# A four-layer encoder on one core: eight pairs of projection groups for six, earlier splits of score banks, and scoring in smaller steps

## The chip, the cores and the metric

The kernel runs on one core of a Trainium2 chip. A core has five engines that work side by side, each with its own instruction stream in a fixed order: TensorE (PE in the profile, with its weight loads shown as PEld), VectorE (DVE), ScalarE (ACT), GpSimd (POOL) and SyncE (SP), whose stream here only issues transfers. Sixteen DMA engines move data between the chip's memory (HBM) and the core's SBUF. The metric is the device time of one execution in microseconds (us); lower is better.

## The reference

Four layers act on a residual stream `x` of 256 tokens by 2048 features, all in float32. Layers 0 and 3 use windowed grouped-query attention, layer 1 a neighbourhood attention on a token grid, layer 2 a differential attention.

```python
for i in range(4):
    h = rmsnorm(x, norm_pre[i])
    proj = h @ w_in[i]             # 2048 x 5120 in layers 0 and 3, 2048 x 8192 in layers 1 and 2
    q, k, v, g = split(proj)
    o = attention_i(q, k, v)       # 16 heads or score maps; one kind of three
    y = (o * silu(g)) @ w_out[i]   # 2048 x 2048
    x = x + rmsnorm(y, norm_post[i])
    x = x + sigmoid(x @ pe_gate[i]) * (p[i] @ pe_proj[i])
```

## The kernel before, in words

**Products in three parts.** Every float32 operand is split into a high part (ACT, a copy into a rounded form) and a low part (DVE, a subtraction): `split`, L108 to L115. `mm3` (L117 to L120) then issues three matmuls: high by high, high by low, low by high. Weights come from HBM in chunks of 128 x 1024 (512 KB), which hold two steps of the contraction for 512 output columns. Tile `wr` holds a raw chunk, `wh` and `wl` its halves.

**Groups and pairs.** A group is 512 output columns: eight chunks, two halves of tokens, so 8 x 2 x 2 x 3 = 96 matmuls of 128 x 512. A group is named by what it yields: `q1` is the second group of queries. Two groups can be joined to a `Pair`, which computes the 2 x 2 block product with seven block products instead of eight: 28 pair chunks of six matmuls. The names are P1 to P7 and E, four chunks each. The weights of P1 and P3 come by a plain transfer into tile `wc`. Those of P5, P7 and P6 are made in place: POOL issues a DMA that adds another block to the tile that has just been split (L228), so P1 is followed by P5, and P3 by P7 and then P6, in the same tile. For E a raw chunk is added by DVE (L221). The order is

```python
PAIR = [("P1", 0), ("P1", 1), ("P1", 2), ("P1", 3), ("P2", 0), ("P5", 0), ("P5", 1), ("P5", 2), ("P5", 3),
        ("P2", 1), ("P2", 2), ("P2", 3)] + [(n, c) for n in ("P3", "P7", "P6", "E") for c in range(4)]
```

**The order of the stream.** `ORDERS` (L42) says for each kind of layer which two groups open it, which pairs follow with which plain groups laid between their chunks, and over how many of those plain chunks the pair is spread (the last number of an entry), and which groups close it. `layer_plan` lays three pair chunks after each eighth plain chunk and spreads the rest evenly over the others. A pair occupies three PSUM banks (`sacc`), plain groups two (`acc`) or two of the three; three more banks (`ps`) serve transposes, scores and values.

**Splits ahead.** The split of a chunk is written four places of the stream ahead of its products (`AHEAD_SPLIT`), in five buffers, so ACT waits until PE has finished the oldest one. There are four buffers each for `wr` and `wc`.

**Steps.** Everything else (attention, transposes, norms) is a queue of short steps. `run_stream` runs one step per plain chunk or per two pair chunks (two when the queue is long). The attention of four heads or maps is started when its q, k and v have arrived: `attend` and `attend_diff`. In them a step `score(p)` makes the scores of two heads or maps, `soft` the exponentials on ACT, `scale` or `blend` the normalisation, `trans` the transposes of the probabilities with their split into `pth` and `ptl`, `value` the product with v. The scheduler of the framework orders each engine's instructions by the place in the program; `tc.high_priority()` lets instructions go ahead of others that are also possible then.

Of the kernel before, what the change touches and what calls it, by code (L numbers as in the profile page):

```python
# [10 lines left out]
F32 = mybir.dt.float32  # L11
# [3 lines left out]
ALU = mybir.AluOpType  # L15
# [24 lines left out]


ORDERS = {  # L42
    0: (["k0", "v0"], [(("q1", "q2"), ["q0", "q3", "g0"], 22)], ["g3", "g1", "g2"]),
    1: (["k0", "q0"], [(("k1", "q1"), ["v0", "v1", "g0"], 22), (("k2", "q2"), ["v2", "g1", "k3"], 20)],
        ["q3", "v3", "g2", "g3"]),
}
ORDERS[2] = ORDERS[1]

# [6 lines left out]
def alibi_slope(h, n):  # L55
    return 2.0 ** (-8.0 * (h + 1) / n)
# [36 lines left out]
def encoder_kernel(ctx: ExitStack, tc: tile.TileContext, t, out):  # L93
# [14 lines left out]
    def split(dst_h, dst_l, src, scale=None):  # L108
        if scale is None:
            A.activation(dst_h, src, AF.Copy)  # L110
            V.tensor_sub(dst_l, src, dst_h.bitcast(F32))  # L111
        else:
            A.activation(dst_h, src, AF.Copy, scale=scale)
            V.scalar_tensor_tensor(dst_l, src, scale, dst_h.bitcast(F32),
                                   op0=ALU.mult, op1=ALU.subtract)  # L115

    def mm3(acc, lh, ll, rh, rl, start, stop, **kw):  # L117
        PE.matmul(acc, lh, rh, start=start, stop=False, **kw)  # L118
# [312 lines left out]
    def acts_of(acts, kt, layer=None, u=None, gain=True):  # L431

        def step():
            if layer is None:
                split(acts.pair(kt, 0), acts.pair(kt, 1), turned(xn[kt // 8], kt % 8 // 2))
                acts.done(kt)
                return
            c = kt % 4
            if not layer:
                for a in range(2):  # L440
                    split(*acts.part(kt + a), u[kt // 4][:, c + a], scale=gpre[:, 0, kt + a:kt + a + 1])
                acts.done(kt)
                return
            ps = turned(xn[kt // 8], kt % 8 // 2)
            if c == 0:
                u.append(work.tile([P, 4, S], F32, name=("s", "snat")[kt // 8]))
            for a in range(2):
                A.activation(u[kt // 4][:, c + a], ps[:, a], AF.Copy, scale=gpre[:, layer, kt + a:kt + a + 1])
            split(acts.pair(kt, 0), acts.pair(kt, 1), u[kt // 4][:, c:c + 2])
            acts.done(kt)  # L450
        return step
# [41 lines left out]
    def turn_heads(dst, i, nat, flag, minus=False):  # L493

        scale = (DH ** -0.5 if i == 1 else 1.0) * (-1 if minus else 1)

        def turn(p):
            def step():
                if not dst:
                    name, bufs = ("kv", 4) if i == 0 else ("q", 2)  # L500
                    for _ in range(2):
                        dst.append(work.tile([P, 4, S], F32R, name=name, bufs=bufs))
                ps = turned(nat, p)
                c = slice(2 * p, 2 * p + 2)
                split(dst[0][:, c], dst[1][:, c], ps, scale=None if scale == 1.0 else scale)
                if p == 1:
                    flags[flag] -= 1
            return step

        flags[flag] = flags.get(flag, 0) + 1  # L510
        steps.extend([idle, turn(0), turn(1)])
# [45 lines left out]
    def turned(nat, p):  # L557

        ps = psp.tile([P, 2, S], F32, name="ps")
        for a in range(2):  # L560
            for m in range(T):
                PE.transpose(ps[:, a, m * P:(m + 1) * P],  # L562
                             nat[:, m, (2 * p + a) * P:(2 * p + a + 1) * P], ident)
        return ps
# [24 lines left out]
    def scores(q, k, qi, ki):  # L589
        ps = psp.tile([P, T, S], F32, name="ps")  # L590
        for m in range(T):
            r = (slice(None), qi, slice(m * P, (m + 1) * P))
            mm3(ps[:, m], q[0][r], q[1][r], k[0][:, ki], k[1][:, ki], True, True)
        return ps

    def probs_T(src_of):

        ps = psp.tile([P, T, S], F32, name="ps")
        for kt in range(T):
            for m in range(T):  # L600
                PE.transpose(ps[:, kt, m * P:(m + 1) * P], src_of(m)[:, kt * P:(kt + 1) * P], ident)  # L601
        h = work.tile([P, T, S], F32R, name="pth")
        l = work.tile([P, T, S], F32R, name="ptl")
        split(h, l, ps)
        return h, l

    def exponentials(s, sink_of=None):
# [17 lines left out]
    def attend(j, q, k, v, k_of, bias_of, sink_of, gs, og_of, after_scores):  # L625

        s = [None, None]
        sums, pt = {}, {}

        def score(p):  # L630
            def step():
                s[p] = work.tile([P, 4, S], F32, name="s")
                for a in range(2):
                    i = 2 * p + a
                    bias_of(s[p][:, a * T:(a + 1) * T], scores(q, k, i, k_of(i)), i)
            return step

        def soft(p):
            def step():
                sums[p] = exponentials(s[p], sink_of(p) if sink_of else None)  # L640
            return step

        def scale(p):
            def step():
                sm, es = sums[p]
                if es is not None:
                    V.tensor_add(sm, sm, es)
                rc = small.tile([P, 4], F32, name="rc")
                V.reciprocal(rc, sm)
                for e in range(4):  # L650
                    A.activation(s[p][:, e], s[p][:, e], AF.Copy, scale=rc[:, e:e + 1])  # L651
            return step

        def trans(i):
            def step():
                pt[i] = probs_T(lambda m: s[i // 2][:, (i % 2) * T + m])
            return step

        def value(i):
            def step():  # L660
                if i % 2 == 0:
                    pt["ps"] = psp.tile([P, 2, S], F32, name="ps")
                ps, (ph, pl) = pt["ps"], pt.pop(i)
                c = slice(k_of(i) * DH, (k_of(i) + 1) * DH)
                for kt in range(T):
                    mm3(ps[:, i % 2], v[0][:, kt, c], v[1][:, kt, c], ph[:, kt], pl[:, kt],
                        kt == 0, kt == T - 1)
                if i % 2 == 1:
                    c = 4 * (j % 2) + i
                    A.activation(og_of(j)[:, c - 1:c + 1], ps, AF.Copy)  # L670
            return step

        def gate(p):
            def step():
                c = 4 * (j % 2) + 2 * p
                og = og_of(j)[:, c:c + 2]
                V.tensor_mul(og, turned(gs[0], p), og)
                if p == 1:
                    flags["gs"] = 0
            return step  # L680

        def both(*fs):
            return lambda: [f() for f in fs]

        return [score(0), both(soft(0), score(1)), both(scale(0), soft(1), after_scores),
                scale(1), trans(0), trans(1), both(value(0), trans(2)),
                both(value(1), trans(3)), value(2), value(3)], [gate(0), gate(1)]

    def attend_diff(j, q, k, v, dist, subln, nlam, lam_init, gs, og_of, after_scores):
# [2 lines left out]
        o = slice(512 * (j % 2), 512 * (j % 2 + 1))  # L692
        ss = small.tile([P, 2, T], F32, name="ss")

        def score(hd):
            def step():
                s[hd] = work.tile([P, 4, S], F32, name="s")
                for a in range(2):
                    ps = scores(q, k, 2 * hd + a, 2 * hd + a)
                    V.scalar_tensor_tensor(s[hd][:, a * T:(a + 1) * T], dist,  # L700
                                           -alibi_slope(2 * j + hd, 8), ps,
                                           op0=ALU.mult, op1=ALU.add)
            return step

        def soft(hd):
            def step():
                sums[hd] = exponentials(s[hd])[0]
            return step
# [16 lines left out]
        def trans(hd):  # L725
            def step():
                pt[hd] = probs_T(lambda m: s[hd][:, m])
            return step
# [35 lines left out]
        def both(*fs):  # L764
            return lambda: [f() for f in fs]

        return [score(0), both(soft(0), score(1)), both(blend(0), soft(1), after_scores),
                blend(1), trans(0), trans(1), value(0), value(1),
                norm], [gate]

    def lambda_of(layer):
# [14 lines left out]
    def layer_plan(layer, hx, sums, xs_last):  # L786
# [69 lines left out]
        def lo_split(j, p):  # L856
            def step():
                kt = 4 * j + 2 * p
                if kind == 2:
                    src = turned(og_of(j), 2 * (j % 2) + p)  # L860
                else:
                    src = og_of(j)[:, kt % 8:kt % 8 + 2]
                split(lo.pair(kt, 0), lo.pair(kt, 1), src)
                lo.done(kt)
            return step

# [291 lines left out]
```

## Time and profile before

| What | Value |
|---|---|
| Median of 3 runs | 2073.7 us (2073.3 to 2075.14) |
| Profiled execution, its own time | 2073.2 us |
| Its span in the profile | 2071.4 us |
| PE busy | 2043.3 us, 99% |
| DVE busy | 1386.4 us, 67% |
| ACT busy | 1226.9 us, 59% |
| Moved by DMA | 428.63 MB, mean 207 GB/s |

The 1.8 us between time and span lie outside the span. A matmul's bar lasts longer than the distance to the next one's start, so the busy time of PE says when it had work in flight, not how much it did; the distance from start to start does. The clock row grants TensorE its higher level (2.4 GHz, shown as 1.00) in every stretch. The input projections are at 5 to 268 us (layer 0), 462 to 848 us (layer 1), 1042 to 1427 us (layer 2) and 1621 to 1876 us (layer 3); output projection and gate lie between them.

### The profile page before, as it was taken

The page shows a single profiled execution, that of the slowest core. Times are in us where ns is not written, and L with a number is a line of the kernel's source. Part 1 is how long each engine was busy: PE and PEld are TensorE (multiplying, and loading weights), DVE is VectorE, ACT ScalarE, POOL GpSimd, SP SyncE. Part 2 cuts the span into 40 slices and gives each one's busy share as a digit, 9 for nine tenths or more (in the row PEclk, how much of TensorE's full clock was granted, in tenths as well). Part 3 has the DMA queues.
Part 4 walks back from the last instruction along what each step waited for, and adds up shares of the span by engine and source line. Part 5 has one row for each costly group of instructions (what it writes and reads, how often), then busy time and mean ns, then how long its engine had stood idle before and what let it go on. Part 6 is the DMA issues. An engine that isn't in the chain of part 4 may idle for free.

```text
span 2071.4 us, 26023 instructions
## 1 busy us (share of the span) xinstructions
PE 2043.3 (99%) x9675; PEld 1690.6 (82%) x9675; DVE 1386.4 (67%) x1603; ACT 1226.9 (59%) x1802; POOL 76.4 (4%) x98
## 2 busy tenths in 40 slices
PE   9999999999999999999999999999999999999999
PEld 6788888888888888888888887888888888888887
DVE  7667755576777776555667787766556767775554
ACT  8567745465657666444656566555545567774543
POOL 0010000000000100000000101000000001000000
PEclk9999999999999999999999999999999999999999
DMA  8875576466788866564667878655656687456744
GB/s 312 261 189 187 174 231 215 154 213 197 224 263 218 237 222 196 194 223 151 208 205 218 247 234 213 226 192 190 217 165 205 209 235 183 153 172 225 223 152 143
DMA packets 125009, 428.63 MB, mean 207 GB/s; under 512 B 13521, under 2 KB 16209, under 8 KB 124881
## 3 DMA queue, kind: packets, MB, share of 16 engines
q1 hardware_dynamic: 114512, 389.21, 56.8%
q0 software_dynamic: 10368, 37.75, 10.4%
q8 instruction: 76, 1.25, 0.2%
q14 instruction: 53, 0.43, 0.1%
HBM read 418.52 MB, written 8.39 MB: 206 GB/s over the span
## 4 chain that ended last, share of the span: by engine, by line
PE 61%; DVE 3%; issue 3%; ACT 2%; DMA 2%; POOL 0%; DVEq 0%; ACTq 0%; POOLq 0%
PE acc L118 10%; PE acc L120 10%; PE acc L119 10%; PE sacc L118 8%; PE sacc L119 8%; PE sacc L120 8%; DMA wr<-in_w_in 2%; PE ps L562 2%; DVE wl L111 1%; ACT wh L110 1%; PE ps L119 1%; PE ps L120 1%; PE ps L118 1%; PE ps L601 1%; ACT s L651 0%
## 5 line engine op out<-in xcount | busy, mean ns | idle before, releaser
L111 DVE TENSOR_TENSOR wl<-wr,wh 128x1024 fp32r<-128x1024 f32 (+1 forms) x605 | 736.7, 1222 | 434.4 <-ACT wh L110 429.7
L110 ACT ACTIVATE wh<-wr 128x1024 fp32r<-128x1024 f32 (+1 forms) x605 | 639.3, 1058 | 584.1 <-PE acc L120 293.0
L118 PE MATMUL acc<-wh,lh 128*128 128x512 f32 x896 | 354.4, 396 | 1.6 <-ACT wh L110 1.3
L119 PE MATMUL acc<-wl,lh 128*128 128x512 f32 x896 | 350.6, 391 | 4.7 <-DVE wl L111 4.7
L120 PE MATMUL acc<-wh,lh 128*128 128x512 f32 x896 | 350.4, 391 | 0.0
L118 PE MATMUL sacc<-wh,ls 128*128 128x512 f32 x664 | 262.2, 395 | 2.7 <-ACT snat L545 2.1
L119 PE MATMUL sacc<-wl,ls 128*128 128x512 f32 x664 | 259.3, 391 | 0.1
L120 PE MATMUL sacc<-wh,ls 128*128 128x512 f32 x664 | 258.9, 390 | 0.0
L110 ACT ACTIVATE wh<-wc 128x1024 fp32r<-128x1024 f32 x144 | 152.4, 1059 | 140.6 <-PE acc L120 103.3
L111 DVE TENSOR_TENSOR wl<-wc,wh 128x1024 fp32r<-128x1024 f32 x144 | 175.8, 1223 | 81.7 <-ACT wh L110 79.6
L118 PE MATMUL sacc<-wh,lh 128*128 128x512 f32 x528 | 210.0, 398 | 2.2 <-ACT wh L110 2.1
L119 PE MATMUL sacc<-wl,lh 128*128 128x512 f32 x528 | 206.7, 391 | 2.5 <-DVE wl L111 2.5
L120 PE MATMUL sacc<-wh,lh 128*128 128x512 f32 x528 | 206.9, 392 | 0.0
L119 PEld LDWEIGHTS acc<-wl,lh 128*128 128x128 f32 x896 | 168.5, 188 | 39.5 <-DVE wl L111 6.8
L118 PE MATMUL acc<-wh,ls 128*128 128x512 f32 x504 | 197.9, 393 | 0.0
L118 PEld LDWEIGHTS acc<-wh,lh 128*128 128x128 f32 x896 | 168.4, 188 | 36.1 <-ACT wh L110 2.0
L120 PEld LDWEIGHTS acc<-wh,lh 128*128 128x128 f32 x896 | 168.3, 188 | 35.1
L119 PE MATMUL acc<-wl,ls 128*128 128x512 f32 x504 | 196.5, 390 | 0.0
L120 PE MATMUL acc<-wh,ls 128*128 128x512 f32 x504 | 196.3, 390 | 0.0
L118 PEld LDWEIGHTS sacc<-wh,ls 128*128 128x128 f32 x664 | 124.8, 188 | 29.1 <-ACT snat L545 3.0
L120 PEld LDWEIGHTS sacc<-wh,ls 128*128 128x128 f32 x664 | 124.7, 188 | 26.2
L119 PEld LDWEIGHTS sacc<-wl,ls 128*128 128x128 f32 x664 | 124.9, 188 | 24.6 <-DVE wl L111 0.5
(227 smaller groups left out, 2501.4 us busy)
## 6 DMA issues: line engine op xcount, KB each, us to landing
wr<-in_w_in SPq DMA_DIRECT2D x367, 512.0 KB, 4.5
wr<-in_w_out SPq DMA_DIRECT2D x128, 512.0 KB, 4.2
wr<-in_pe_gate SPq DMA_DIRECT2D x128, 512.0 KB, 3.9
wc<-in_w_in POOLq DMA_DIRECT2D x72, 512.0 KB, 7.2
wc<-in_w_in SPq DMA_DIRECT2D x48, 512.0 KB, 4.7
wr<-in_pe_proj SPq DMA_DIRECT2D x16, 512.0 KB, 4.7
xs<-lx SPq DMA_DIRECT2D x12, 512.0 KB, 3.8
lx<-xs SPq DMA_DIRECT2D x12, 512.0 KB, 5.3
```

Source lines behind the costliest of these rows:

```text
L110: A.activation(dst_h, src, AF.Copy)
L111: V.tensor_sub(dst_l, src, dst_h.bitcast(F32))
L118: PE.matmul(acc, lh, rh, start=start, stop=False, **kw)
L119: PE.matmul(acc, lh, rl, start=False, stop=False, **kw)
L120: PE.matmul(acc, ll, rh, start=False, stop=stop, **kw)
L562: PE.transpose(ps[:, a, m * P:(m + 1) * P], nat[:, m, (2 * p + a) * P:(2 * p + a + 1) * P], ident)
L601: PE.transpose(ps[:, kt, m * P:(m + 1) * P], src_of(m)[:, kt * P:(kt + 1) * P], ident)
```

## The change

Three things change. In layers 1 and 2 `ORDERS` now has three pairs (k1 with q1, k2 with q2, k3 with q3) for two, each spread over 15 of the 16 plain chunks beside it; in layers 0 and 3 the one pair is spread over 21 plain chunks instead of 22. Splits whose source is a `ps` bank (and one DVE product from such a bank) are issued with high priority. A scoring step makes one head or map instead of two; the scaling or blending of the second half and the first transposes become one step. From L112 on, lines of the changed kernel have numbers that are 4 to 6 higher.

```diff
 ORDERS = {
-    0: (["k0", "v0"], [(("q1", "q2"), ["q0", "q3", "g0"], 22)], ["g3", "g1", "g2"]),
-    1: (["k0", "q0"], [(("k1", "q1"), ["v0", "v1", "g0"], 22), (("k2", "q2"), ["v2", "g1", "k3"], 20)],
-        ["q3", "v3", "g2", "g3"]),
+    0: (["k0", "v0"], [(("q1", "q2"), ["q0", "q3", "g0"], 21)], ["g3", "g1", "g2"]),
+    1: (["k0", "q0"], [(("k1", "q1"), ["v0", "v1"], 15), (("k2", "q2"), ["g0", "v2"], 15),
+                      (("k3", "q3"), ["g1", "v3"], 15)], ["g2", "g3"]),
 }
...
+    def split_now(*args, **kw):
+        with tc.high_priority():
+            split(*args, **kw)
...
-                split(dst[0][:, c], dst[1][:, c], ps, scale=None if scale == 1.0 else scale)
+                split_now(dst[0][:, c], dst[1][:, c], ps, scale=None if scale == 1.0 else scale)
...
-        split(h, l, ps)
+        split_now(h, l, ps)
...
-        def score(p):
-            def step():
-                s[p] = work.tile([P, 4, S], F32, name="s")
-                for a in range(2):
-                    i = 2 * p + a
-                    bias_of(s[p][:, a * T:(a + 1) * T], scores(q, k, i, k_of(i)), i)
+        def score(p, a):
+            def step():
+                if a == 0:
+                    s[p] = work.tile([P, 4, S], F32, name="s")
+                i = 2 * p + a
+                bias_of(s[p][:, a * T:(a + 1) * T], scores(q, k, i, k_of(i)), i)
...
-        return [score(0), both(soft(0), score(1)), both(scale(0), soft(1), after_scores),
-                scale(1), trans(0), trans(1), both(value(0), trans(2)),
+        return [score(0, 0), score(0, 1), both(soft(0), score(1, 0)), score(1, 1), both(scale(0), soft(1), after_scores),
+                both(scale(1), trans(0)), trans(1), both(value(0), trans(2)),
                 both(value(1), trans(3)), value(2), value(3)], [gate(0), gate(1)]
```

The same is done in `attend_diff`, and the other three uses of `split` on a `ps` bank are replaced too.

Three places show how instructions move. The first is ACT in layer 0, the second attention: `wh` are weight splits, `s` the scores, `pth` the high part of transposed probabilities. Before:

```order
113 L617 ACTIVATE s,sm<-s,ng 128x256 x4
114 L622 ACTIVATE es<-es 128x4
115 L110 ACTIVATE wh<-wr 128x1024
116 L110 ACTIVATE wh<-wc 128x1024
117 L651 ACTIVATE s<-s,rc 128x256 x4
118 L617 ACTIVATE s,sm<-s,ng 128x256 x4
119 L622 ACTIVATE es<-es 128x4
120 L110 ACTIVATE wh<-wc 128x1024
121 L651 ACTIVATE s<-s,rc 128x256 x4
122 L110 ACTIVATE pth<-ps 128x512
123 L110 ACTIVATE wh<-wr 128x1024
124 L110 ACTIVATE pth<-ps 128x512
```

The same place of the changed kernel:

```order
113 L621 ACTIVATE s,sm<-s,ng 128x256 x4
114 L626 ACTIVATE es<-es 128x4
115 L110 ACTIVATE wh<-wr 128x1024
116 L655 ACTIVATE s<-s,rc 128x256 x4
117 L110 ACTIVATE wh<-wr 128x1024
118 L621 ACTIVATE s,sm<-s,ng 128x256 x3
119 L110 ACTIVATE pth<-ps 128x512
120 L621 ACTIVATE s,sm<-s,ng 128x256
121 L626 ACTIVATE es<-es 128x4
122 L110 ACTIVATE wh<-wr 128x1024
123 L655 ACTIVATE s<-s,rc 128x256 x3
124 L110 ACTIVATE pth<-ps 128x512
```

The first `pth` has moved ahead of the last exponential and of the second scaling, which stood before it.

The second is DVE in layer 1 where the first pair ends: `wl<-wr` are splits of plain chunks, `wl<-wc` those of pair chunks, `wc<-wc,wr` the additions for E, `ptl` the low parts of transposed probabilities. Before:

```order
376 L111 TENSOR_TENSOR wl<-wr,wh 128x1024
377 L221 TENSOR_TENSOR wc<-wc,wr 128x1024
378 L111 TENSOR_TENSOR wl<-wc,wh 128x1024
379 L111 TENSOR_TENSOR wl<-wr,wh 128x1024
380 L221 TENSOR_TENSOR wc<-wc,wr 128x1024
381 L111 TENSOR_TENSOR wl<-wc,wh 128x1024
382 L111 TENSOR_TENSOR wl<-wr,wh 128x1024
383 L221 TENSOR_TENSOR wc<-wc,wr 128x1024
384 L111 TENSOR_TENSOR wl<-wc,wh 128x1024
385 L221 TENSOR_TENSOR wc<-wc,wr 128x1024
386 L111 TENSOR_TENSOR wl<-wr,wh 128x1024
387 L111 TENSOR_TENSOR wl<-wc,wh 128x1024 x2
```

The same pair's end in the changed kernel:

```order
358 L225 TENSOR_TENSOR wc<-wc,wr 128x1024
359 L111 TENSOR_TENSOR ptl<-ps,pth 128x512
360 L653 RECIPROCAL rc<-sm 128x4
361 L111 TENSOR_TENSOR wl<-wc,wh 128x1024
362 L111 TENSOR_TENSOR ptl<-ps,pth 128x512
363 L225 TENSOR_TENSOR wc<-wc,wr 128x1024
364 L111 TENSOR_TENSOR wl<-wr,wh 128x1024
365 L111 TENSOR_TENSOR wl<-wc,wh 128x1024
366 L111 TENSOR_TENSOR ptl<-ps,pth 128x512 x2
367 L111 TENSOR_TENSOR wl<-wc,wh 128x1024
368 L225 TENSOR_TENSOR wc<-wc,wr 128x1024
369 L111 TENSOR_TENSOR wl<-wr,wh 128x1024
```

Fewer plain splits stand between the additions, and the four `ptl` of the first attention have come in among them.

The third is POOL in layer 2, which issues the adding DMAs (`wc<-in_w_in2` by its place) and computes a power for the attention's norm (`ro`), in one queue. Before:

```order
22 L420 TENSOR_TENSOR rstd<-v,mhalf 128x2
23 L228 DMA wc<-in_w_in 128x1024 x9
24 L750 TENSOR_TENSOR ro<-ss,mhalf 128x4
25 L228 DMA wc<-in_w_in 128x1024 x7
26 L750 TENSOR_TENSOR ro<-ss,mhalf 128x4
27 L228 DMA wc<-in_w_in 128x1024 x8
28 L750 TENSOR_TENSOR ro<-ss,mhalf 128x4 x2
```

The same stretch of the changed kernel:

```order
22 L424 TENSOR_TENSOR rstd<-v,mhalf 128x2
23 L232 DMA wc<-in_w_in 128x1024 x12
24 L756 TENSOR_TENSOR ro<-ss,mhalf 128x4
25 L232 DMA wc<-in_w_in 128x1024 x9
26 L756 TENSOR_TENSOR ro<-ss,mhalf 128x4
27 L232 DMA wc<-in_w_in 128x1024 x12
28 L756 TENSOR_TENSOR ro<-ss,mhalf 128x4
29 L232 DMA wc<-in_w_in 128x1024 x3
30 L756 TENSOR_TENSOR ro<-ss,mhalf 128x4
```

There are 36 adding DMAs for 24; two of the powers, for one, now stand behind the ninth DMA of a pair with three more of that pair behind them.

## Rows read from the trace of the kernel before

**Rows 1.** The page, part 1: busy time, share of the span, instructions.

```profile
span 2071.4 us, 26023 instructions
PE 2043.3 (99%) x9675; PEld 1690.6 (82%) x9675; DVE 1386.4 (67%) x1603; ACT 1226.9 (59%) x1802; POOL 76.4 (4%) x98
```

**Rows 2.** Windows by stage: length, busy time (instructions) of engines, clock, DMA.

```profile
5.00:268.00 263.00, 254.46 (x1256) 209.94 (x1255) 192.90 (x260) 184.76 (x319) 12.72 (x14) 1.00 0.74 229
268.00:462.00 194.00, 193.69 (x884) 159.59 (x883) 117.02 (x120) 102.08 (x136) 0.72 (x1) 1.00 0.63 200
462.00:848.00 386.00, 381.76 (x1840) 317.92 (x1840) 275.52 (x306) 243.88 (x347) 21.83 (x26) 1.00 0.74 218
...
1042.00:1427.00 385.00, 378.65 (x1807) 313.96 (x1806) 278.62 (x339) 235.40 (x348) 26.26 (x30) 1.00 0.72 216
...
1621.00:1876.00 255.00, 253.47 (x1266) 212.03 (x1265) 181.49 (x231) 168.49 (x275) 11.81 (x14) 1.00 0.66 193
```

**Rows 3.** Timeline of PE from 880 us: start, length, instruction.

```profile
880.02 0.39 PE L118 MATMUL acc<-wh,ls 128*128 128x512 f32 x1
...
892.26 0.39 PE L118 MATMUL acc<-wh,ls 128*128 128x512 f32 x1
```

**Rows 4.** Waits of PE in the whole span: total us, times, longest us.

```profile
PE acc L119 <- DVE wl L111: 4.7, 5, 2.9
PE sacc L119 <- DVE wl L111: 2.5, 3, 1.0
PE sacc L118 <- ACT snat L545: 2.1, 3, 0.7
...
PE ps L118 <- ACT pth L110: 1.5, 2, 0.8
```

**Rows 5.** Groups by form: count | busy us, mean ns | idle before, releasers.

```profile
L111 DVE TENSOR_TENSOR wl<-wr,wh 128x1024 fp32r<-128x1024 f32 x603 | 735.3, 1224 | 433.7 <-ACT wh L110 429.1
L110 ACT ACTIVATE wh<-wr 128x1024 fp32r<-128x1024 f32 x603 | 638.1, 1060 | 583.8 <-PE acc L120 293.0 <-PE sacc L120 230.3 <-issue 40.9
...
L221 DVE TENSOR_TENSOR wc<-wc,wr 128x1024 f32<-128x1024 f32 x24 | 29.2, 1223 | 13.9 <-DMA wr<-in_w_in 13.5
...
L538 DVE SCALAR_TENSOR_TENSOR snat<-sacc,rstd,snat 128x512 f32<-128x512 f32 x24 | 17.4, 745 | 0.0
...
L551 DVE TENSOR_TENSOR snat<-snat 128x512 f32<-128x512 f32 x6 | 4.1, 684 | 0.0
```

**Rows 6.** The adding DMAs (L228): POOL's ns min/median/max, then transfer to landing.

```profile
L228 POOL DMA_DIRECT2D wc<-in_w_in x72: 862/862/1047, 53.1 to 1738.4; - x72
...
DMA to landing us min/median/max: 5.2/7.2/11.3
```

**Rows 7.** Windows inside the pairs' stretches of layers 1 and 2.

```profile
660.00:710.00 50.00, 49.90 (x236) 41.47 (x235) 37.47 (x37) 32.78 (x38) 6.93 (x8) 1.00 0.93 249
...
1190.00:1240.00 50.00, 48.76 (x235) 40.15 (x234) 41.49 (x54) 32.38 (x48) 3.45 (x4) 1.00 0.78 228
1240.00:1290.00 50.00, 48.32 (x220) 38.88 (x218) 34.44 (x37) 32.88 (x44) 7.99 (x9) 1.00 0.83 224
1290.00:1340.00 50.00, 48.12 (x232) 40.02 (x232) 39.94 (x51) 28.99 (x44) 0.00 (x0) 1.00 0.64 221
```

**Rows 8.** Timeline of PE in layer 0, the second attention, with idle time before.

```profile
170.55 0.38 PE L118 MATMUL ps<-pth,kv 128*128 128x256 f32 x1 [0.78 <-ACT pth L110]
171.28 0.38 PE L119 MATMUL ps<-ptl,kv 128*128 128x256 f32 x1 [0.34 <-DVE ptl L111]
```

**Rows 9.** DMA issues: instruction, count, size, median us to landing.

```profile
wc<-in_w_in POOLq DMA_DIRECT2D x72, 512.0 KB, 7.2
```

More of the change, by code (lines that the diff above doesn't have):

```diff
@@ L434, in step @@
             if layer is None:
-                split(acts.pair(kt, 0), acts.pair(kt, 1), turned(xn[kt // 8], kt % 8 // 2))
+                split_now(acts.pair(kt, 0), acts.pair(kt, 1), turned(xn[kt // 8], kt % 8 // 2))
                 acts.done(kt)
@@ L676, in step @@
                 og = og_of(j)[:, c:c + 2]
-                V.tensor_mul(og, turned(gs[0], p), og)
+                ps = turned(gs[0], p)
+                with tc.high_priority():
+                    V.tensor_mul(og, ps, og)
                 if p == 1:
@@ L693, in attend_diff, with score @@
         ss = small.tile([P, 2, T], F32, name="ss")
-        def score(hd):
+        def score(hd, a):
             def step():
[L697 to L702, printed above, removed]
+                if a == 0:
+                    s[hd] = work.tile([P, 4, S], F32, name="s")
+                ps = scores(q, k, 2 * hd + a, 2 * hd + a)
+                V.scalar_tensor_tensor(s[hd][:, a * T:(a + 1) * T], dist,
+                                       -alibi_slope(2 * j + hd, 8), ps,
+                                       op0=ALU.mult, op1=ALU.add)
             return step
@@ L765, in both @@
             return lambda: [f() for f in fs]
-        return [score(0), both(soft(0), score(1)), both(blend(0), soft(1), after_scores),
-                blend(1), trans(0), trans(1), value(0), value(1),
+        return [score(0, 0), score(0, 1), both(soft(0), score(1, 0)), score(1, 1), both(blend(0), soft(1), after_scores),
+                both(blend(1), trans(0)), trans(1), value(0), value(1),
                 norm], [gate]
@@ L862, in step @@
                     src = og_of(j)[:, kt % 8:kt % 8 + 2]
-                split(lo.pair(kt, 0), lo.pair(kt, 1), src)
+                split_now(lo.pair(kt, 0), lo.pair(kt, 1), src)
                 lo.done(kt)
```

## The prediction

> **What bounds the kernel now.** I read the page's first part, then windows by stage, then PE's own waits, then the pairs' stretches. The first part shows PE with work in flight for 2043.3 of 2071.4 us, DVE for 67% and ACT for 59% of the span [rows 1]. PE idles 28.1 us in all. The windows say where [rows 2]: 263.00 - 254.46 = 8.5 us in the input projection of layer 0, 4.2 in that of layer 1, 6.4 in layer 2, 1.5 in layer 3; between layers 0 and 1 only 0.3 in 194 us. So the idle time sits where pairs and attention are mixed, and the rest of the program is a row of matmuls without holes.
>
> What a matmul is worth is not its bar of 0.39 us. From the L118 row at 880.02 to the one at 892.26 there are 54 starts in 12.24 us [rows 3]: 0.2267 us each. A plain chunk (12 matmuls) holds PE for 2.72 us and a pair chunk (6) for 1.36.
>
> **The change part by part.**
>
> *Two more pairs.* Two groups as plain ones are 2 x 96 = 192 matmuls, as a pair 28 x 6 = 168. Two more pairs, one each in layers 1 and 2, take away 48 matmuls of 128 x 512. PE is the engine that everything waits for here, so they count in full: 48 x 0.2267 = 10.9 us. The transposes that turn the results move from `nat` to `snat` with the same count.
>
> The Trainium skill (TensorE: Matmul & The Clock Gate, Back-to-back issue gap) gives about 131 ns for each 512-column matmul in a sustained stream of weight loads and matmuls; the gain would be 48 x 0.131 = 6.3 us by that estimate. The trace does not agree: 226.7 ns in a stretch without a hole [rows 3], and the measurement decides.
>
> *What the pairs add.* Each pair has 28 splits for 16, so 12 more on ACT (1.06 us) and DVE (1.22 us), 4 additions for E (1.22 us) and a longer drain of its banks (4 of 0.745 us and one of 0.684) [rows 5]. DVE gets 12 x 1.224 + 4 x 1.223 + 3.7 = 23.3 us more per layer, ACT 12 x 1.06 = 12.7. DVE in layer 1 then works 275.5 + 23.3 = 298.8 us of about 381 (386 less half of 10.9): 78% after 71% [rows 2]. That lies beside PE's work as long as the splits stay ahead. POOL issues 24 more adding DMAs of 512 KB [rows 9]; plain transfers keep their number, so 12.6 MB more are moved, 3% of 428.6.
>
> *The denser stretch.* Before, 22 pair chunks were spread over 20 or 18 plain chunks; now 25 over 14, 1.79 to one. Four pair chunks and what lies between them last 4 x 1.36 + 2.24 x 2.72 = 11.5 us on PE, where they lasted 14.3 (18 plain) to 15.3 us (20). Three things must fit into these 11.5 us. (a) DVE while E runs: 4 x (1.224 + 1.223) + 2.24 x 1.224 = 12.5 us, so it falls 1.0 us behind; before it needed 13.8 of 14.3. The reserve is the four chunks split ahead, 4 x 11.5/6.24 = 7.4 us of PE's time. (b) One round of the adding chain (split, add, next split of the same tile): 1.06 + 1.22 + 7.2 us to landing at the median [rows 5, 6] = 9.5. It fits by 2 us; with the longest landing, 11.3, it is 13.6 and late by 2.1. (c) DMA: the share was 0.93 at 249 GB/s in the densest 50 us, with PE idle for only 0.1 us of them [rows 7]; the mean over a whole mix changes little, since a third of its plain chunks left with the time.
>
> The price of extra waiting, from both sides. At best none: the densest window of DMA cost PE nothing. From the nearest count: layers 1 and 2 wait 4.2 + 6.4 = 10.6 us with four pairs, 2.65 a pair, so two more cost 5.3. At worst the chain of (b) is late in each round (below). I take 3 us, nearer to the row per pair, because some of today's waits there belong to attention, which gets better.
>
> *Score banks first, one head to a step.* No instruction is added but the steps: one more per attention. PE waits for `pth` and `ptl` at 170.55 and 171.28 us for 0.78 and 0.34 us [rows 8]; the transposed bank stood behind exponentials and scalings on ACT. With the first `pth` moved ahead of them, and the scores of two heads no longer in one burst on DVE, such waits shrink. Their kind totals 1.5 us over the whole span in the row of `pth` [rows 4], and some of the 7.2 us that PE waits for `wl` there stems from the same bursts of scoring. Bounds: a loss of the 1.22 us of a weight split that is now behind, once per attention at worst and only where the reserve of 7.4 us is gone; a gain of at most the 10.0 us of layers 0 and 3, of which the chip's start is a part that stays. I take -2 us. Spreading over 21 instead of 22 plain chunks in layers 0 and 3 leaves PE's work as it is; I cost it at nothing, covered by the same reserve.
>
> *The tail.* With two closing groups for four, less plain work follows the last scores in layers 1 and 2: 16 plain chunks are 43.5 us after the pair's end. The last attention needs about 18 steps (turns, 11 of attention), one or two to a chunk, and its result is first wanted six chunks into the output projection. It fits; no price.
>
> *Sum.* -10.9 + 3 - 2 = -9.9 us on the profiled 2073.2: 2063.3. The median of the runs is 0.5 above the profiled one, so 2063.8, rounded to 2064.
>
> **The rivals.**
>
> *A, the adding chain becomes the bound (slower).* In P7 and P6 a tile's next split needs the landing of a DMA issued one round earlier. If landings go to the 11.3 us of the longest row, each of the two rounds in each of the six pairs of layers 1 and 2 is 2.1 us late; where bursts on DVE have used the reserve, that is 12 x 2.1 = 25 us on PE: 2073.7 - 10.9 + 25.2 = 2088. It turns into a loss from 10.9/12 = 0.9 us late, that is from a mean landing of 11.5 + 0.9 - 2.3 = 10.1 us with the reserve spent. For it: windows near full DMA share exist already [rows 7], POOL's queue holds a norm ahead of three adding DMAs twice in layer 2, and 24 more are issued. Against it: the median is 7.2 and the reserve is 7.4.
>
> The Trainium skill (SBUF — State Buffer, Who interferes with whom) adds that a DVE instruction with two SBUF inputs blocks a GpSimd one that reads SBUF for its whole length, which would speak against more adding DMAs beside more splits; 24 x 1.22 us would be put into the chain by such a block. This trace shows no sign of it: POOL's issue took 862 ns at the least and at the median, 1047 at most [rows 6].
>
> *B, DVE's load eats the gain (about the same).* In 50 us windows with DVE at 80 to 83% PE idled 1.2 to 1.9 us, 2.5 to 3.8% [rows 7]. The three mixes of a layer last about 3 x (16 x 2.72 + 28 x 1.36) = 245 us of dense work and some 27 of attention; both layers 544 us. At 3.8% that is 20.7 us where there are 10.6: +10.1, and 2073.7 - 10.9 + 10.1 = 2072.9. For it: E now asks more of DVE than the time holds, and the first attention falls into it. Against it: the two windows' waits are partly for a bank's drain, not for DVE.
>
> *C, the waits mostly vanish (faster still).* If scoring in small steps takes away half the 20.6 us of idle time in the four projections beside keeping the pairs free, at most some -8 beyond the matmuls: 2073.7 - 10.9 - 8 = 2054.8. Against it: most waits there are single ones under 1 us with a different cause each [rows 4].
>
> *That the pairs don't take the matmuls away* can be left out: the counts above are those of the program.
>
> **How the numbers follow.** The forecast (2064, from 2058 to 2069) 0.64; A 0.09; B, with a half gain, 0.18; C 0.09. Runs of this kernel differ by up to 0.1%, so 0.2% (4.1 us) is about what can be told from no change: faster below 2069.6, slower above 2077.8. Faster is the forecast, C and a third of B: 0.79; same is most of B and the small losses of A: 0.13; slower is the rest of A and of B: 0.08. The range leaves out most of A and the far end of C: 2056 to 2074.
>
> **What would show it.** PE should have 48 fewer matmuls and the same 0.2267 us between starts in a full stretch; DVE about 45 us and ACT about 25 us more busy time; idle time of PE in layers 1 and 2 between 8 and 18 us in sum, in layers 0 and 3 below 9. The waits for `pth` and `ptl` should shrink. A is right if ACT's `wh` waits for the landing of `wc` by tens of us in sum and landings of L232 have a median over 9; B if PE waits for `wl` far longer than 7.2 us while DVE is above 90% in the E stretches. The forecast is wrong if idle time in layers 1 and 2 grows by more than 7 us, or if it falls by more than 6.

## The result and the profile after

The changed kernel takes 2093.62 us (median of 4 runs, 2091.59 to 2095.51; the profiled one took 2095.51) where the kernel before took 2074.42 beside it: 1.0093 times as long, with a 95% interval of [1.0081, 1.0105]. The forecast was 2064 us, in a range of 2056 to 2074. It had the sign wrong.

In rows of the changed kernel the lines from L117 of the kernel before on have numbers that are 4 to 6 higher; L110 to L114 are the same in both. First part of the page of the changed kernel, and its row of the adding DMAs (count, size, median us to landing):

```profile
span 2093.7 us, 26098 instructions
PE 2052.1 (98%) x9627; PEld 1693.1 (81%) x9627; DVE 1433.0 (68%) x1645; ACT 1251.8 (60%) x1826; POOL 98.7 (5%) x122
...
wc<-in_w_in POOLq DMA_DIRECT2D x96, 512.0 KB, 8.0
```

The counts are those forecast: PE has 48 matmuls fewer than in [rows 1], DVE works 46.6 us longer, ACT 24.9, and 24 adding DMAs more are issued. So the work is as expected, and the time was lost beside it. The windows by stage of the changed kernel show where (length; busy us and instructions of PE, PEld, DVE, ACT, POOL; granted clock; DMA share; GB/s):

```profile
5.00:268.00 263.00, 256.71 (x1257) 211.53 (x1256) 195.52 (x260) 184.89 (x319) 12.71 (x14) 0.99 0.74 229
...
462.00:861.00 399.00, 384.96 (x1809) 317.85 (x1808) 295.72 (x323) 254.15 (x356) 32.25 (x38) 0.98 0.80 228
1055.00:1450.00 395.00, 381.18 (x1780) 314.59 (x1779) 296.88 (x353) 245.12 (x347) 37.12 (x41) 0.98 0.80 227
1644.00:1898.00 254.00, 253.89 (x1266) 211.68 (x1265) 184.34 (x232) 168.45 (x275) 11.79 (x14) 1.00 0.65 193
```

Against [rows 2]: layer 0 has the same length, layer 3 is 1 us shorter, layers 1 and 2 are 13 and 10 us longer, although each lost 24 matmuls (5.4 us). Read to a hundredth from the timeline, from their first matmul to the first of the output projection, they are 12.5 and 9.0 longer; the loss to explain is 12.5 + 9.0 + 10.9 = 32.4 us. PE's idle time there is 14.0 + 13.8 = 27.9 us, after 4.2 + 6.4 = 10.6. That is 17.3 of the 32.4. The clock column says where to look for more: 0.98 where it was 1.00.

PE's waits in the changed kernel over the whole span (total us, times, longest us):

```profile
PE ps L566 <- DVE snat L542: 11.0, 8, 3.1
PE acc L123 <- DVE wl L111: 6.7, 6, 2.8
PE sacc L122 <- DVE snat L542: 4.7, 4, 1.3
PE ps L566 <- DVE snat L555: 3.7, 6, 1.5
PE sacc L123 <- DVE wl L111: 2.1, 3, 1.0
```

Three of the five rows have to do with `snat`, the buffer into which a pair's three banks (`sacc`) are drained: 11.0 + 4.7 + 3.7 = 19.4 us. In the kernel before, the same waits (its L562 and L118 behind L538) are 2.0 and 0.6:

```profile
PE ps L562 <- DVE snat L538: 2.0, 3, 1.5
...
PE sacc L118 <- DVE snat L538: 0.6, 2, 0.3
```

The waits for `wl`, at which rival B pointed, grew only from 7.2 to 8.8.

**One pair's end, before and after.** PE's timeline of the kernel before at the first pair's end of layer 1 (start, length, instruction):

```profile
617.74 0.39 PE L120 MATMUL sacc<-wh,lh 128*128 128x512 f32 x1
617.97 0.39 PE L118 MATMUL acc<-wh,lh 128*128 128x512 f32 x1
...
623.41 0.38 PE L562 MATMUL ps<-ident,snat 128*128 128x128 f32 x2
```

E's last matmul into `sacc` starts at 617.74. Two plain chunks into `acc` follow, 24 matmuls, and at 623.41 the first transposes that turn `snat` find their data (a later one waits 0.25 us). PE worked for 5.4 us while the banks were drained. PE's timeline of the changed kernel at the third pair's end of layer 1 (in brackets the idle time before, and what ended it):

```profile
795.31 0.39 PE L124 MATMUL sacc<-wh,lh 128*128 128x512 f32 x1
795.54 0.39 PE L122 MATMUL acc<-wh,lh 128*128 128x512 f32 x1
...
798.03 0.39 PE L124 MATMUL acc<-wh,lh 128*128 128x512 f32 x1
798.26 0.38 PE L566 MATMUL ps<-ident,snat 128*128 128x128 f32 x2
801.70 0.45 PE L566 MATMUL ps<-ident,snat 128*128 128x128 f32 x1 [3.06 <-DVE snat L542]
803.41 0.90 PE L566 MATMUL ps<-ident,snat 128*128 128x128 f32 x3 [1.27 <-DVE snat L555]
805.30 0.77 PE L122 MATMUL sacc<-wh,lh 128*128 128x512 f32 x1 [0.99 <-DVE snat L542]
...
806.71 0.63 PE L122 MATMUL sacc<-wh,lh 128*128 128x512 f32 x1
807.14 0.63 PE L123 MATMUL sacc<-wl,lh 128*128 128x512 f32 x1
...
811.54 0.39 PE L123 MATMUL sacc<-wl,lh 128*128 128x512 f32 x1
811.77 0.40 PE L124 MATMUL sacc<-wh,lh 128*128 128x512 f32 x1
```

Only one plain chunk follows (12 matmuls, 795.54 to 798.03), since the pair is spread over 15 of 16. Then PE waits three times, 5.3 us in all, first to turn `snat` and then for the banks themselves, which the next user wants. Behind the waits the matmuls start 0.43 us apart and not 0.2267 [rows 3]: the granted clock has fallen from 2.4 to 1.2 GHz. At 811.54 they are back at 0.23.

Why the drain takes that long stands in the queues of ACT and DVE of the changed kernel, same pair's end:

```profile
797.92 1.06 ACT L110 ACTIVATE wh<-wr 128x1024 fp32r<-128x1024 f32 x1 [1.47 <-DMA wr<-in_w_in]
798.88 0.67 ACT L552 ACTIVATE snat<-sacc,rstd 128x512 f32<-128x512 f32 x1
```

```profile
799.01 1.22 DVE L111 TENSOR_TENSOR wl<-wr,wh 128x1024 fp32r<-128x1024 f32 x1 [1.30 <-ACT wh L110]
800.15 1.40 DVE L542 SCALAR_TENSOR_TENSOR snat<-sacc,rstd,snat 128x512 f32<-128x512 f32 x2
801.53 1.23 DVE L111 TENSOR_TENSOR wl<-wr,wh 128x1024 fp32r<-128x1024 f32 x1
802.67 0.69 DVE L555 TENSOR_TENSOR snat<-snat 128x512 f32<-128x512 f32 x1
803.27 1.22 DVE L111 TENSOR_TENSOR wl<-wr,wh 128x1024 fp32r<-128x1024 f32 x1
804.40 0.75 DVE L542 SCALAR_TENSOR_TENSOR snat<-sacc,rstd,snat 128x512 f32<-128x512 f32 x1
```

ACT's copy out of the bank, possible from about 795.7, stands behind a weight split that waits for its transfer, and starts at 798.88. On DVE each part of the drain stands behind another weight split. So 0.67 us on ACT and 1.40 + 0.69 + 0.75 on DVE are spread over 9 us. The drain was hardly shorter before: from the start of E's last matmul to the end of the last addition it took 6.2 to 8.0 us at the four pair ends of layers 1 and 2 then, and takes 6.5 to 9.8 at the six now. What differs is the plain work behind the end: 5.4 us or more before, 2.7 now.

Windows of the changed kernel at the six pair ends:

```profile
600.00:610.00 10.00, 7.66 (x32) 5.89 (x31) 7.89 (x11) 4.95 (x7) 1.73 (x2) 0.83 0.92 198
700.00:710.00 10.00, 8.82 (x35) 7.19 (x36) 5.80 (x9) 4.46 (x6) 0.86 (x1) 0.83 0.98 242
800.00:810.00 10.00, 6.05 (x15) 4.45 (x16) 7.16 (x10) 3.98 (x5) 0.00 (x0) 0.56 0.59 201
1190.00:1200.00 10.00, 7.60 (x31) 5.71 (x30) 8.21 (x11) 4.94 (x8) 2.66 (x3) 0.86 1.01 243
1290.00:1300.00 10.00, 7.60 (x24) 5.72 (x23) 7.20 (x10) 4.81 (x7) 1.58 (x2) 0.66 1.01 243
1390.00:1400.00 10.00, 6.83 (x22) 5.14 (x23) 6.25 (x9) 4.12 (x6) 0.00 (x0) 0.66 0.51 173
```

The granted clock is below 0.9 at all six, and at 1.00 in the windows of the kernel before [rows 7]. Counted in the timeline, 43 matmuls at these six ends start 0.43 us before the next: 43 x 0.2 = 9 us. With the 17.3 us of idle time that makes 26 of the 32.4 us; the rest is not separated (transposes and first matmuls at the lower clock). An estimate that takes them in: by the six windows the lower level was granted for 32 us in all (3.4 of the 10 us where the clock is 0.83), PE stood idle in about 6 of these by the timeline, and 26 us of work at 0.43 us for 0.2267 are 12 us lost. That leaves 3 us open. The Trainium skill (TensorE: Matmul & The Clock Gate, Loop structure matters more than you think) sketches a loop in which copying a result out of PSUM does not cost PE its clock. These rows show the case in which it does: where the next work needs that copy or its bank.

### The profile page after: what moved, and what is told of

Its sections match the earlier page's. It is cut to its first block, busy times and chain, and to the rows that moved or that the text cites. A ratio compares the mean times of both kernels' runs of the same rounds, so it can differ in the third digit from the quotient of the medians.

```text
span 2093.7 us, 26098 instructions
## 1 busy us (share of the span) xinstructions
PE 2052.1 (98%) x9627; PEld 1693.1 (81%) x9627; DVE 1433.0 (68%) x1645; ACT 1251.8 (60%) x1826; POOL 98.7 (5%) x122
## 4 chain that ended last, share of the span: by engine, by line
PE 81%; DMA 7%; DVE 5%; issue 4%; ACT 3%; SPq 0%; DVEq 0%; POOL 0%; ACTq 0%; POOLq 0%
PE acc L123 12%; PE acc L122 12%; PE acc L124 12%; PE sacc L122 12%; PE sacc L124 12%; PE sacc L123 12%; DMA wr<-in_w_in 4%; DVE wl L111 3%; PE ps L566 2%; DMA wc<-in_w_in 2%; ACT wh L110 2%; PE ps L122 1%; PE ps L123 1%; PE ps L124 1%; PE ps L605 1%
## 5 line engine op out<-in xcount | busy, mean ns | idle before, releaser
L111 DVE TENSOR_TENSOR wl<-wr,wh 128x1024 fp32r<-128x1024 f32 (+1 forms) x581 | 706.9, 1222 | 403.5 <-ACT wh L110 398.7
L110 ACT ACTIVATE wh<-wr 128x1024 fp32r<-128x1024 f32 (+1 forms) x581 | 613.9, 1058 | 556.1 <-PE sacc L124 239.2
L123 PE MATMUL acc<-wl,lh 128*128 128x512 f32 x832 | 327.7, 394 | 6.7 <-DVE wl L111 6.7
L122 PE MATMUL acc<-wh,lh 128*128 128x512 f32 x832 | 329.4, 396 | 0.4 <-ACT wh L110 0.2
L124 PE MATMUL acc<-wh,lh 128*128 128x512 f32 x832 | 325.5, 391 | 0.0
L110 ACT ACTIVATE wh<-wc 128x1024 fp32r<-128x1024 f32 x192 | 202.7, 1059 | 156.0 <-PE acc L124 91.6
L122 PE MATMUL sacc<-wh,ls 128*128 128x512 f32 x728 | 289.1, 397 | 1.7 <-ACT snat L549 1.7
L123 PE MATMUL sacc<-wl,ls 128*128 128x512 f32 x728 | 284.7, 391 | 0.4 <-DVE wl L111 0.4
L124 PE MATMUL sacc<-wh,ls 128*128 128x512 f32 x728 | 284.2, 390 | 0.0
L111 DVE TENSOR_TENSOR wl<-wc,wh 128x1024 fp32r<-128x1024 f32 x192 | 233.6, 1222 | 69.6 <-ACT wh L110 65.4
L122 PEld LDWEIGHTS acc<-wh,lh 128*128 128x128 f32 x832 | 157.0, 189 | 33.6 <-ACT wh L110 1.1
L124 PEld LDWEIGHTS acc<-wh,lh 128*128 128x128 f32 x832 | 156.8, 189 | 32.2
L122 PEld LDWEIGHTS sacc<-wh,ls 128*128 128x128 f32 x728 | 137.0, 188 | 29.9 <-ACT snat L549 4.1
L124 PEld LDWEIGHTS sacc<-wh,ls 128*128 128x128 f32 x728 | 136.8, 188 | 29.1
```

Source lines behind the costliest of these rows:

```text
L123: PE.matmul(acc, lh, rl, start=False, stop=False, **kw)
L124: PE.matmul(acc, ll, rh, start=False, stop=stop, **kw)
```

## The experiments

Three theories stood against each other. **T1:** the table leaves the drain of a pair with one plain chunk, PE waits and the clock falls. **T2:** high priority for the score banks' splits pushes weight splits and drains back. **T3:** the denser stretch (DVE, adding DMAs) is itself too slow. All times are medians, and ratios stand against the kernel before on the same chip.

**The new table alone**, in the kernel before:

```diff
-    1: (["k0", "q0"], [(("k1", "q1"), ["v0", "v1", "g0"], 22), (("k2", "q2"), ["v2", "g1", "k3"], 20)],
-        ["q3", "v3", "g2", "g3"]),
+    1: (["k0", "q0"], [(("k1", "q1"), ["v0", "v1"], 15), (("k2", "q2"), ["g0", "v2"], 15),
+                      (("k3", "q3"), ["g1", "v3"], 15)], ["g2", "g3"]),
```

(and 21 for 22 in layers 0 and 3).

> The kernel before with the new ORDERS table alone: three pairs in layers 1 and 2, no high priority, scoring steps of two heads. Theory T1 (the drain of a pair's three banks takes 4.5 to 8 us and has only one plain chunk of 2.7 us beside it at each pair's end; PE stands, and its clock falls to the lower level for some us after) expects 2088 to 2098, with six stalls of PE at the pairs' ends as in the changed kernel. Theory T2 (the high priority of other splits pushes the drain back on DVE) expects no such stalls and about 2064. Theory T3 (the adding chain or DVE's load in the denser stretch) expects about 2094, with waits spread over the pairs and not at their ends.

Measured: 2096.51 us (2094.01 to 2101.03), 1.0102 [1.0085, 1.0119]. The whole loss comes with the table. Its waits of PE:

```profile
PE ps L562 <- DVE snat L538: 8.4, 6, 3.3
PE sacc L118 <- DVE snat L538: 7.3, 6, 1.3
PE ps L562 <- DVE snat L551: 5.3, 6, 3.0
```

These are 21.0 us, six times each. T2 falls.

**The old table** in the changed kernel (the same diff the other way round).

> The changed kernel with the old ORDERS table: six pairs, but high priority and one head to a scoring step. T1 expects 2066 to 2074 (nothing lost, some us of attention waits gone). T2 expects 2080 or more, with stalls at the pairs' ends. T3 expects 2070 to 2074.

Measured: 2075.63 (2072.27 to 2078.06, 10 runs), 1.0003 [0.9994, 1.0013]. Priority and small steps do no harm, which agrees with T1, but with the old table they are worth nothing either, just outside what was expected.

**The pairs over 13 plain chunks**, nothing else:

```diff
-    1: (["k0", "q0"], [(("k1", "q1"), ["v0", "v1"], 15), (("k2", "q2"), ["g0", "v2"], 15),
-                      (("k3", "q3"), ["g1", "v3"], 15)], ["g2", "g3"]),
+    1: (["k0", "q0"], [(("k1", "q1"), ["v0", "v1"], 13), (("k2", "q2"), ["g0", "v2"], 13),
+                      (("k3", "q3"), ["g1", "v3"], 13)], ["g2", "g3"]),
```

It makes the stretch denser and leaves three plain chunks behind the end, so T1 and T3 want opposite signs.

> The changed kernel with each pair of layers 1 and 2 spread over 13 plain chunks instead of 15, so that three plain chunks (8.2 us) stand between a pair's end and the next pair's first product; everything else as changed, and the pairs' stretch denser still. T1 expects the stalls at the pairs' ends gone and 2056 to 2068. T2 expects 2088 to 2096. T3 expects it slower than the changed kernel: 2094 to 2105.

Measured: 2056.85 (2051.69 to 2059.12), 0.9905 [0.9888, 0.9923], which is 36.8 us below the changed kernel, at the near end of what T1 expected. Its windows of layers 1 and 2, and of PE's waits that for the drained `snat`:

```profile
462.00:842.00 380.00, 375.96 (x1811) 312.72 (x1810) 293.11 (x323) 251.81 (x357) 32.29 (x38) 1.00 0.82 240
1036.00:1412.00 376.00, 373.25 (x1779) 310.00 (x1778) 293.97 (x352) 242.50 (x352) 35.78 (x41) 1.00 0.82 239
```

```profile
PE ps L566 <- DVE snat L542: 1.4, 2, 1.2
```

Both layers are 19 us shorter than in the changed kernel with nearly the same work on DVE, ACT and POOL; PE's idle time is 6.8 us for 27.9, the clock is back at 1.00. T3 falls for a spread of 13.

**The drain ahead of the weight splits**: the other way to take the wait away.

```diff
-        return {("P5", 3): after_p5, ("P2", 3): after_p2, ("P7", 3): after_p7, ("E", 3): after_e}
+        return {("P5", 3): after_p5, ("P2", 3): after_p2, ("P7", 3): after_p7, ("E", 3): urgent(after_e)}
```

> The changed kernel with the drain after E (ACT copy and DVE additions) issued with high priority. Two splits of 1.2 us no longer stand between its instructions, so it lasts about 3.7 us instead of 5 to 6. T1 expects stalls about 2 us shorter each and a clock that falls less often: 2068 to 2086. T2 expects about 2064. T3 expects 2090 to 2096, no change beyond noise.

Measured: 2078.53 (2076.11 to 2083.9, 10 runs), 1.0018 [1.0008, 1.0028]: 15.1 us of the loss are gone. Windows at the second and the third pair's end of layer 1:

```profile
690.00:700.00 10.00, 8.75 (x45) 6.96 (x44) 9.86 (x13) 7.43 (x10) 2.60 (x3) 1.00 1.03 301
787.00:803.00 16.00, 11.14 (x44) 8.50 (x43) 10.56 (x13) 7.34 (x10) 0.00 (x0) 0.79 0.63 245
```

That lies in T1's range. At four of the six ends ACT now starts the drain 0.04 us behind the end of E's last matmul, one wait of 1.3 us is left there, and PE keeps its clock (shown for the second end). At the third end of each layer a split that waits for its transfer is already in the queue, and the drain is 3.9 and 2.2 us late. A better place in the queue helps; it doesn't replace work behind the end.

**14, 11 and 12 plain chunks** (the diff of 13 with other numbers): how much cover is needed, and where the density begins to bind.

> The changed kernel with the pairs of layers 1 and 2 spread over 14 plain chunks: two plain chunks (5.4 us) stand behind a pair's end, as in the kernel before. T1 (a drain of 4.5 to 8 us has to be covered) expects most of the stalls gone, some of 0 to 2 us left: 2058 to 2072, between 15 (2094) and 13 (2057) and nearer to 13. A theory by density alone (13 faster than 15 because work is pulled forward) expects a value halfway, about 2075.

> The changed kernel with the pairs spread over 11 plain chunks: five plain chunks (13.6 us) behind each pair's end, and 25 pair chunks over 10 plain ones before it. T1 expects no stall at the pairs' ends and nothing more gained there than with 13. The rivals of the prediction (adding chain, DVE's load) would now decide: four pair chunks and 1.6 plain ones last 9.8 us, against 9.5 us of the chain at a landing of 7.2: 2060 to 2080 if they bind, 2055 to 2059 if they do not.

> The changed kernel with the pairs over 12 plain chunks: four plain chunks (10.9 us) behind the end, four pair chunks and 1.76 plain ones last 10.2 us. T1 with the adding chain as the other limit expects a value between 13 (2057) and 11 (2093.5): 2060 to 2085, with waits for the drain of P7 (the ACT copy into snat, which stands behind splits that wait for adding DMAs) and none at the pairs' ends.

| Spread over | Plain chunks behind the end | Median us (range) | Ratio |
|---|---|---|---|
| 15 (the change) | 1 | 2093.62 (2091.59 to 2095.51) | 1.0093 [1.0081, 1.0105] |
| 14 | 2 | 2069.7 (2062.48 to 2072.21) | 0.9971 [0.996, 0.9983] |
| 13 | 3 | 2056.85 (2051.69 to 2059.12) | 0.9905 [0.9888, 0.9923] |
| 12 | 4 | 2055.34 (2054.12 to 2057.92) | 0.9915 [0.9898, 0.9932] |
| 11 | 5 | 2093.5 (2091.21 to 2095.71) | 1.0095 [1.0079, 1.0111] |

With 14 the time lies in T1's range, and the theory by density alone expected about 2075. The turns wait 1.4 us; what is longest now is the drain at P7's end, earlier in the pair:

```profile
PE sacc L122 <- ACT snat L549: 6.3, 3, 2.7
```

So the pairs' ends no longer explain most of the 13 us between 14 and 13. What does is not shown: P7's drain is one part, and the clock fell in other places too.

With 11 I expected 2060 to 2080 if the dense stretch binds. It went past that, with no stall left at the pairs' ends. PE's waits, PE's timeline and ACT's timeline with 11:

```profile
PE sacc L122 <- ACT snat L549: 18.9, 4, 6.6
```

```profile
771.46 0.80 PE L122 MATMUL sacc<-wh,ls 128*128 128x512 f32 x1 [3.16 <-ACT snat L549]
```

```profile
768.25 1.06 ACT L110 ACTIVATE wh<-wc 128x1024 fp32r<-128x1024 f32 x1 [1.14 <-DMA wc<-in_w_in]
...
770.73 0.68 ACT L549 ACTIVATE snat<-sacc,rstd 128x512 f32<-128x512 f32 x1
```

A weight split that waits for the landing of an adding DMA stands ahead of P7's drain (L549) on ACT, and PE waits for that drain's bank. In sum ACT waits 39.8 us for such landings, after 9.3 in the kernel before. That is rival A's chain, but it reaches PE through a drain behind the late split. With 12 it does not bind, against my expectation of 2060 to 2085: the step lies between 12 and 11.

**The spread of 13 with parts of the change.** In the kernel before, with the table alone:

```diff
-    1: (["k0", "q0"], [(("k1", "q1"), ["v0", "v1", "g0"], 22), (("k2", "q2"), ["v2", "g1", "k3"], 20)],
-        ["q3", "v3", "g2", "g3"]),
+    1: (["k0", "q0"], [(("k1", "q1"), ["v0", "v1"], 13), (("k2", "q2"), ["g0", "v2"], 13),
+                      (("k3", "q3"), ["g1", "v3"], 13)], ["g2", "g3"]),
```

> The kernel before with three pairs over 13 plain chunks (and the one of layers 0 and 3 over 21), without high priority and with scoring steps of two heads. T1 expects that the order of the pairs carries nearly all: 2056 to 2064, against 2057 with the other two edits.

Measured: 2071.01 (2061.56 to 2073.74, 10 runs), 0.9973 [0.9957, 0.999]. The waits for the drained `snat` are small (3.9 us to turn it), but 14 us are missing against the run with all parts: T1 alone does not forecast this one. So the other two edits do matter in the dense table. Which of them, two more runs tell. With the one-head steps, without priority (nor for the DVE product from a `ps` bank), against the changed kernel with 13:

```diff
-        with tc.high_priority():
-            split(*args, **kw)
+        split(*args, **kw)
```

> Pairs over 13 plain chunks and one head or map to a scoring step, without the high priority. If the scoring bursts on DVE are what separates 2071 (table alone) from 2057 (all), it comes to 2054 to 2062; if the priority is, to 2066 to 2073.

Measured: 2061.49 (2059.21 to 2067.66), 0.9945 [0.9926, 0.9964]. And with priority, without the one-head steps (cut: `attend_diff` and the old lists of steps come back too):

```diff
-        def score(p, a):
+        def score(p):
             def step():
-                if a == 0:
-                    s[p] = work.tile([P, 4, S], F32, name="s")
-                i = 2 * p + a
-                bias_of(s[p][:, a * T:(a + 1) * T], scores(q, k, i, k_of(i)), i)
+                s[p] = work.tile([P, 4, S], F32, name="s")
+                for a in range(2):
+                    i = 2 * p + a
+                    bias_of(s[p][:, a * T:(a + 1) * T], scores(q, k, i, k_of(i)), i)
```

> Pairs over 13 plain chunks and the high priority for splits of ps banks, with scoring steps of two heads. If the priority is what separates 2071 (table alone) from 2057 (all), it comes to 2054 to 2062; if the scoring bursts are, to 2066 to 2073.

Measured: 2069.87 (2062.65 to 2072.24, 10 runs), 0.9972 [0.996, 0.9984]. By the medians the steps bring 9.5 us from the table alone (2071.01), priority 1.1, which is within the runs' spread, and both 14.2. The steps probably carry most of it. That is not firm: the intervals of the table alone and of the steps overlap, the chips' kernels before differ by 1 us, and some 4 us come only with both edits.

**13 and the drain first**, both diffs from above.

> Pairs over 13 plain chunks and the drain after E with high priority, on top of the changed kernel. T1: with 8.2 us behind the pair's end the drain is covered already, so the priority adds little: 2052 to 2060, against 2057 with 13 alone.

Measured: 2057.01 (2055.07 to 2058.62), 0.9918 [0.9904, 0.9933]. As T1 has it: where the drain is covered, its place in the queue is worth nothing.

**Filler for PE**: how much of the loss is the clock? Behind each pair's drain in layers 1 and 2, 32 transposes of the identity into a bank that nothing reads (`fill` is true in these layers):

```diff
+            ps = psp.tile([P, T, S], F32, name="ps")
+            for _ in range(32 if pair.fill else 0):
+                PE.transpose(ps[:, 0, :P], ident, ident)
             then(*n)
```

> The changed kernel with 32 transposes of the identity (108 ns each, 3.5 us) put on PE behind the drain of each of the six pairs of layers 1 and 2, just ahead of the transposes that wait for it; their result is not used. If half of the loss is the clock that falls behind each stall (the profile of the changed kernel shows 56 matmuls at 0.43 instead of 0.23 us, 11 us), PE keeps its clock and the time falls to 2078 to 2088 though PE has 21 us more work. If the stall alone is the loss, the filler lies in it and the time stays at 2091 to 2097; if the filler does not lie in the stall, it rises to 2100 or more.

Measured: 2092.85 (2090.26 to 2096.23), 1.0087 [1.007, 1.0105], no gain. (The 56 matmuls and 11 us of this expectation are a count over the whole program; at the six ends there are 43, 9 us.) PE's timeline with the filler at the first pair's end of layer 1, and the windows there and at the third:

```profile
606.21 3.66 PE L559 MATMUL ps<-ident 128*128 128x128 f32 x32
609.71 0.62 PE L569 MATMUL ps<-ident,snat 128*128 128x128 f32 x4
```

```profile
600.00:610.00 10.00, 10.00 (x64) 8.82 (x63) 8.29 (x10) 5.40 (x6) 2.38 (x3) 1.00 0.86 240
...
805.00:815.00 10.00, 5.88 (x27) 4.79 (x26) 7.00 (x9) 3.40 (x5) 0.00 (x0) 0.83 0.64 209
```

The clock stayed at 1.00 at five of the six ends, but the filler holds PE for about 3.5 us at each, 21 us in all, and the next matmul into the banks comes no earlier: 6.6 to 10.7 us behind the start of E's last one, after 6.6 to 10.0. The time lies in the range that was written for the stall alone, but it can't be read so. The waits for `snat` fell only from 19.4 to 6.8 us, so the filler lies in the stalls in part. And this execution lost time elsewhere: in layer 1, ahead of the first pair's end, PE waited 2.55 us for a weight split, after 1.30, and 13 matmuls behind it started 0.43 us apart. Layer 2, where the clock stayed at 1.00, became 4.4 us shorter than in the changed kernel, although PE had 10.5 us more to do there; layer 1 became 2.7 us longer. So the split of the loss between waiting and clock stays as counted, 17 and some 9 us or more, and is not shown by an experiment.

The best versions, 12 and 13, beat both kernels: about 18 us (0.9%) below the kernel before.

## Why the prediction was wrong

- **The matmuls taken away (-10.9 us): right.** 48 fewer, and in a full stretch they start 0.2267 us apart. With 12 or 13, where the new stalls are gone, the whole gain and more appears.
- **The work that is added: right.** 46.6 us on DVE and 24.9 on ACT, forecast about 45 and 25.
- **"What the pairs add ... a longer drain of its banks": the step that failed.** I priced the drain as 3.7 us of DVE's work that "lies beside PE's work as long as the splits stay ahead", and named the splits as cover. The drain's own cover is the plain work between a pair's last chunk and the next need of its banks and of `snat`. The diff showed it: 22 of 24 and 20 of 24 leave two and four plain chunks, 15 of 16 leaves one, 2.7 us. Nor did I take the drain's length from E's last matmul to the last addition, which the trace of before had at 6.2 us and more; busy time is not delay where a queue is in order.
- **"I take 3 us" for extra waiting: measured 17.3 of idle time, and a loss of 32.4 in all.** The clock has 9 to 12 us of the difference, counted and not tested. The 2.65 us a pair that I drew from the rows of waits came from pairs with more cover. And I priced a wait as its own length; here the clock fell behind it.
- **The tail: priced at the wrong end.** I counted plain chunks after the last scores of a layer, not those after each pair. The layer's tail itself fits, as forecast: the last attention's work reaches into the output projections, which are 1.2 and 1.0 us longer by it, and PE waits for none of it.
- **Scores first and one-head steps (-2 us): near in layers 0 and 3, but by luck.** These gave 1.5 us, in which the spread of 21 for 22 has a part that was not tested alone; the `pth` waits are gone, but the `ptl` waits are 1.2 us for 0.7. With the old table both edits are worth nothing, with the pairs over 13 they are worth 14 us: their size depends on the table, which no term of the sum had.
- **Rival A was not the cause at 15, though its time (2088) was near.** Of its two signs one failed: landings rose to 8.0 us at the median, not above 9, as the adding DMAs of the changed kernel show:

```profile
DMA to landing us min/median/max: 5.2/8.0/12.7
```

  The other came: ACT's waits for them rose from 9.3 to 29.8 us. But they are 24.9 and 29.6 us with 13 and 12 plain chunks too, where the stretch is denser and the kernel faster, so they mostly did not reach PE. At 11 a form of A decides.
- **Rival B** asked for waits for `wl` far above 7.2 us; they are 8.8. **Rival C**'s 2055 is close to what 12 and 13 reach, with fewer stalls in layers 1 and 2 as it said, but not by this change.
- **The sign of failure was the right one:** idle time in layers 1 and 2 growing by more than 7 us. It grew by 17.3.

## What to carry to other kernels

Where an accumulator is drained, ask what PE does between its last matmul and the next need of the same bank or of the drained data, and set that against the drain's delay in its in-order queues, not against its busy time. A schedule that "spreads over N of M" should be read for the M - N left behind, and tried at several N: here 15, 13 and 11 cost 2094, 2057 and 2094 us with the same work, at 11 for another reason, the dense stretch. A wait that ends a full stream of matmuls costs more than its length when the clock falls behind it.

## What the runs showed of the hardware

- In the changed kernel, two or three waits of 2.3 to 5.3 us in all, in an otherwise full stream, went with a granted clock of 0.56 to 0.86 in the 10 us windows at all six pair ends; matmuls then start 0.43 us apart for some microseconds (806.71 to 810.6 above). It was not so each time: with the table alone the first end of layer 1 had 2.4 us of waits and a clock of 1.00, and with the drain first four ends with one wait of 1.3 us kept 1.00.
- 32 transposes of an identity, 128 x 128 in float32, took 3.66 us (0.11 us each); put where PE had waited, they went with a clock of 1.00 at five of six ends.
- Twenty-four more adding DMAs of 512 KB, in a denser stretch, moved the median landing from 7.2 [rows 6] to 8.0 us and the longest from 11.3 to 12.7; POOL's issue stayed at 862 ns at the median.
